# A hybrid transformer block on one core: weight buffers and normalised inputs that begin at different offsets

## The chip, the cores and the metric

The kernel runs on one core of a Trainium2 chip. The metric is the device time of one execution in microseconds. Three runs of the kernel before gave 820.04, 820.05 and 821.41 us, median 820.05 us. The profiled execution is a fourth one, of 820.38 us, and its trace spans 818.3 us from the first instruction to the last.

## The reference, cut to what matters

One block of a network for 512 tokens of width 1024, in float32. What counts here is which products of matrices there are; the rest hangs between them.

```python
u  = rms_norm(h, mix_norm_g)
z  = u @ w_in                              # 1024 -> 512 + 3*768 + 2*1024
y_a = s5_mixer(z[..., :512], ...) @ w_branch_a
y_b = dilated_attention(q, k, v) @ w_branch_b
h  = h + (g_a * y_a + g_b * y_b) @ w_out   # g_a, g_b: sigmoids of the last 2048 columns of z
u2 = rms_norm(h, ffn_norm_g)
gate = causal_depthwise_conv(u2 @ ffn_w_gate, ffn_conv_w, ffn_conv_b)
h  = h + (gelu(gate) * (u2 @ ffn_w_up)) @ ffn_w_down
u3 = rms_norm(h, ple_norm_g)
h  = h + sigmoid(u3 @ ple_w_gate) * (p @ ple_w_proj)
return rms_norm(h, final_norm_g)
```

## The kernel before

Activations lie with their features on the 128 partitions and the 512 tokens along the free axis; a width of 1024 is eight such slices (k = 0 to 7). The five engines work side by side and wait for one another by semaphores, which the tile framework places.

Each product is made in float32 accuracy out of three matmuls in the one-pass float32r format. Every operand is split into a high part, which is the value copied into a float32r tile, and a low part, which is what is left over. `mm3` (L148 to L151) then adds high times high (L149), high times low (L150) and low times high (L151) into one bank of PSUM. A matmul has a stationary operand of 128 columns, which TensorE loads first (the rows called PEld, LDWEIGHTS), and a moving operand that streams past it, here of 512 columns, in the last two output slices of 256.

Weights come in chunks of 1024 columns. `wprep` (L118 to L132) fetches one over SyncE's DMA queue into `wr`, ScalarE copies it into `wh` (L128), and VectorE subtracts into `wl` (L129). Each of the three has three buffers that are used in turn, and `wchunk` asks for the next chunk long before TensorE needs it. There are 130 chunks. The first 20 belong to the token-major products (`proj_tok`), in which the weights are the moving operand and the input `u1` is stationary: 24 matmuls a chunk, into tiles named `pa`. In the other 110 (`gemm`) 128 columns of weights are stationary and the activations move: eight weight tiles a chunk, three matmuls each. The last 16 weight tiles are used for two halves of the tokens, which adds 48. That makes 20 x 24 + 110 x 24 + 48 = 3168 matmuls of this kind, 3072 of them 512 columns wide and 96 of them 256 wide.

The normalised inputs `u1`, `u2` and `u3` share one set of four tiles (`u_tiles`, L153): `uh0` and `uh1` for the high parts, `ul0` and `ul1` for the low ones, each with four slices of 512 columns. `u_split` (L158) fills them. They are operands of `pa`, `v`, `gps` (the gates), `pg` and `pu` (the feed-forward block's two input products) and `eps` (the last gate). The other products read `mh`, `ml`, `ah`, `al`, `zh`, `zl`, `yh`, `yl`, `bx` and `px_`, which this kernel keeps in other slots; `zh` and `zl` reuse the slots of `uh0` and `ul0`.

All these tiles come out of two pools one behind the other, and their sizes per partition are whole multiples of 2048 bytes (8192 for a part of `u`, 4096 for a weight buffer). The order of allocation places them so that every one of those 3168 matmuls has both operands at the same distance, 64 bytes, past a multiple of 256 bytes. Slices within a tile start at multiples of 512 bytes and change nothing in that. An exception among the float32r matmuls are four others, in `rstd_full` (L241 and L242, twice): their stationary operand is `ones_r`, a small tile that lies 160 bytes past a multiple of 256, and 32 past a multiple of 64.

Between the products stand float32 matmuls (transposes, the recurrence's, attention), VectorE's work on the recurrence (`E`, `scr`), softmax, the convolution and the norms. None of it is touched.

Of the kernel before, what the change touches and what calls it, by code (L numbers as in the profile page):

```python
# [10 lines left out]
F32R = mybir.dt.float32r  # L11
# [6 lines left out]
P = 128  # L18
D = 1024
KD = D // P  # L20
SEQ = 512
# [22 lines left out]
STATS_AT = (7, 0)  # L44
NLAST = 2
LAST = ((0, 1), (2, 3))
LN2_HI = 0.693359375
LN2_LO = -2.12194440e-4

# [15 lines left out]
def tile_hybrid_block(ctx: ExitStack, tc: tile.TileContext, xT, xtok, pT, W, vecs, consts, ssm, out):  # L65
# [6 lines left out]
    ring = ctx.enter_context(tc.tile_pool(name="ring", bufs=3))  # L72
# [3 lines left out]
    def slot(i, shape, name, dt=F32):  # L76
        return sb.tile([P] + shape, dt, tag=f"s{i}", name=name)
# [10 lines left out]
    def t_tile(name):  # L88
        return ring.tile([P, 512], F32, tag="t", name=name, bufs=4)
# [22 lines left out]
    def wchunk():  # L112
        if ready:
            return ready.pop(0)
        with ahead():
            return wprep()

    def wprep(pieces=1, after=None):  # L118
        i = wpos[0]
        wpos[0] += 1  # L120
        raw = ring.tile([P, 1024], F32, tag="wr", name=f"wr{i}", bufs=3)
        hi = ring.tile([P, 1024], F32R, tag="wh", name=f"wh{i}", bufs=3)
        lo = ring.tile([P, 1024], F32R, tag="wl", name=f"wl{i}", bufs=3)
        n = 1024 // pieces
        for j in range(pieces):
            c = slice(j * n, (j + 1) * n)
            nc.sync.dma_start(raw[:, c], W[i][:, c])
            ACT.activation(hi[:, c], raw[:, c], AF.Copy)  # L128
            DVE.tensor_tensor(lo[:, c], raw[:, c], hi[:, c].bitcast(F32), op=ALU.subtract)  # L129
            if after and j == 0:  # L130
                after()
        return hi, lo  # L132
# [18 lines left out]
        PE.matmul(ps, st[1], mv[0], start=False, stop=last)  # L151

    def u_tiles(name):  # L153
        uh = [slot(f"uh{j}", [4, SEQ], f"{name}h{j}", F32R) for j in range(2)]
        ul = [slot(f"ul{j}", [4, SEQ], f"{name}l{j}", F32R) for j in range(2)]
        return ([uh[k // 4][:, k % 4, :] for k in range(KD)], [ul[k // 4][:, k % 4, :] for k in range(KD)])

    def u_split(u, k, src, gcol, c=slice(0, SEQ)):  # L158
# [13 lines left out]
    def first():  # L172
        for c in (slice(0, 128), slice(128, SEQ)):
            nc.sync.dma_start(x[:, 0, c], xT[:, 0, c])
            u_split(u, 0, x[:, 0, :], V_MIX, c)

    u = u_tiles("u1")
    ready.append(wprep(2, first))
    load_x(1)
    load_x(2)  # L180
    ready.append(wprep(2))
    load_x(3)
    nc.sync.dma_start(sp, ssm)
# [237 lines left out]
    def stt(o, a, s, b, o0, o1):  # L421
        DVE.scalar_tensor_tensor(o, a, s, b, op0=o0, op1=o1)

    def g_ssm():
# [12 lines left out]
        def rint(o, a, s):  # L437
            ts(o, a, s, ALU.mult, MAGIC, ALU.add)
            ts(o, o, -MAGIC, ALU.add)

        def exp_(o, a):
            xx, n, n1, r, q = e1, e2, e3, e4, e5
            ts(xx, a, -170.0, ALU.max, 170.0, ALU.min)
            rint(n, xx, LOG2E)
            stt(r, n, -LN2_HI, xx, ALU.mult, ALU.add)
            stt(r, n, -LN2_LO, r, ALU.mult, ALU.add)
# [448 lines left out]
    for m in range(4):  # L895
        ps = mm_tile("lps")
        gemm(ps, 4, (parts(yh, 4), parts(yl, 4)))
        t = t_tile("lg")
# [8 lines left out]
    h = slot("x", [KD, SEQ], "h")  # L907
# [21 lines left out]


    u2 = u_tiles("u2")
    acc2 = sb.tile([P, SEQ], F32, tag="acc", name="acc2")
    for m in range(KD):
# [11 lines left out]
    for part in range(2):  # L945
# [4 lines left out]
        for mi in range(HALF):  # L950
# [10 lines left out]
            t = t_tile("cv")  # L961
# [9 lines left out]
        if part == 1:  # L971
            u3 = u_tiles("u3")
            acc3 = sb.tile([P, SEQ], F32, tag="acc", name="acc3")
# [74 lines left out]
    waiting = []  # L1048
    for gi, rs in enumerate(LAST):
        c = slice(rs[0] * 128, rs[-1] * 128 + 128)  # L1050
        end = gi == len(LAST) - 1
        for m in tail:
# [19 lines left out]
    n = 0  # L1072
    for rs, y in zip(LAST, y4):
        for j in range(2):
# [153 lines left out]
```

## Time and profile before

| | |
|---|---|
| median of three runs | 820.05 us |
| the profiled execution | 820.38 us |
| its span | 818.3 us |
| TensorE busy (PE) | 801.2 us, 98% |
| weight loads (PEld) | 664.3 us, 81%, beside the matmuls |
| VectorE busy | 508.5 us, 62% |
| ScalarE busy | 346.4 us, 42% |
| mean granted TensorE clock | 0.987 |

A matmul is listed with the time from its start to its modelled end, 389 ns for 512 columns, and the next one starts before that end. So the pace of TensorE is read from the distance of two starts and not from the busy time.

### The profile page before, as it was taken

The numbers are of one execution on the slowest core, as the hardware profiler recorded it, in microseconds if no ns is written. First come the engines' busy times: TensorE is split into PE (matmuls) and PEld (weight loads), VectorE is DVE, ScalarE is ACT, GpSimd is POOL, SyncE is SP. The second block draws the span as 40 slices with busy tenths as digits, with TensorE's granted clock in tenths as the row PEclk, the third lists the DMA queues.
The fourth block names the chain that finished last, engine by engine and source line by source line (L and its number), as shares of the span: only waits on it lengthen the run. The fifth ranks groups of instructions, "written<-read, shape, count | busy, mean of one in ns | idle before, by whom it ended". The sixth has DMA issues, their size and how long they took to land.

```text
span 818.3 us, 10848 instructions
## 1 busy us (share of the span) xinstructions
PE 801.2 (98%) x4294; PEld 664.3 (81%) x4294; DVE 508.5 (62%) x944; ACT 346.4 (42%) x543; POOL 10.9 (1%) x10
## 2 busy tenths in 40 slices
PE   9999989799999999999999999999999999999996
PEld 7888868589777788888888888888888888888886
DVE  7963999992354447855776555332565556445586
ACT  6773632335344434344354433222344434335454
POOL 2001000000000000000000000000000000000000
PEclk9999998799999999999999999999999999999999
DMA  7731111122111123442322233223322332233202
GB/s 279 269 99 57 51 53 59 70 82 74 53 52 53 53 78 103 139 153 96 128 98 85 101 103 104 88 92 104 103 94 88 104 103 87 95 103 103 81 23 103
DMA packets 23810, 78.97 MB, mean 97 GB/s; under 512 B 2640, under 2 KB 3024, under 8 KB 23760
## 3 DMA queue, kind: packets, MB, share of 16 engines
q1 hardware_dynamic: 23616, 78.22, 28.2%
q8 instruction: 33, 0.54, 0.3%
q14 instruction: 17, 0.14, 0.1%
q10 hardware_dynamic: 144, 0.07, 0.0%
HBM read 76.18 MB, written 2.10 MB: 96 GB/s over the span
## 4 chain that ended last, share of the span: by engine, by line
PE 86%; DVE 10%; ACT 2%; issue 1%; DMA 0%; DVEq 0%; ACTq 0%
PE pg L151 5%; PE pu L151 5%; PE dps L150 5%; PE dps L151 5%; PE pu L150 5%; PE pu L149 5%; PE pg L150 5%; PE pg L149 5%; PE dps L149 5%; PE gps L149 4%; PE gps L151 4%; PE gps L150 4%; DVE E L413 3%; DVE scr L413 2%; PE pa L150 2%; PE pa L151 2%
## 5 line engine op out<-in xcount | busy, mean ns | idle before, releaser
L128 ACT ACTIVATE wh<-wr 128x1024 fp32r<-128x1024 f32 (+1 forms) x132 | 138.1, 1047 | 297.7 <-issue 61.6
L129 DVE TENSOR_TENSOR wl<-wr,wh 128x1024 fp32r<-128x1024 f32 (+1 forms) x132 | 160.0, 1213 | 68.2 <-ACT wh L128 67.9
L150 PE MATMUL pu<-u2l,wh 128*128 128x512 f32 x176 | 68.5, 389 | 0.0
L149 PE MATMUL pu<-u2h,wh 128*128 128x512 f32 x176 | 68.5, 389 | 0.0
L151 PE MATMUL pg<-u2h,wl 128*128 128x512 f32 x176 | 68.5, 389 | 0.0
L149 PE MATMUL pg<-u2h,wh 128*128 128x512 f32 x176 | 68.5, 389 | 0.0
L150 PE MATMUL pg<-u2l,wh 128*128 128x512 f32 x176 | 68.5, 389 | 0.0
L149 PE MATMUL dps<-ah,wh 128*128 128x512 f32 x176 | 68.5, 389 | 0.0
L150 PE MATMUL dps<-al,wh 128*128 128x512 f32 x176 | 68.5, 389 | 0.0
L151 PE MATMUL dps<-ah,wl 128*128 128x512 f32 x176 | 68.5, 389 | 0.0
L151 PE MATMUL pu<-u2h,wl 128*128 128x512 f32 x176 | 68.5, 389 | 0.0
L150 PE MATMUL pa<-wl,u1h 128*128 128x512 f32 x160 | 63.3, 396 | 0.4 <-DVE u1l L160 0.4
L149 PE MATMUL pa<-wh,u1h 128*128 128x512 f32 x160 | 63.5, 399 | 0.2 <-ACT u1h L159 0.2
L151 PE MATMUL pa<-wh,u1l 128*128 128x512 f32 x160 | 62.7, 394 | 0.0
L149 PE MATMUL gps<-u1h,wh 128*128 128x512 f32 x128 | 51.3, 401 | 0.0
L151 PE MATMUL gps<-u1h,wl 128*128 128x512 f32 x128 | 50.5, 394 | 0.0
L150 PE MATMUL gps<-u1l,wh 128*128 128x512 f32 x128 | 50.2, 392 | 0.0
L413 DVE TENSOR_TENSOR ext<-pg,n_y 128x512 f32<-128x512 f32 x22 | 15.2, 692 | 44.1 <-PE pg L151 44.1
L413 DVE TENSOR_TENSOR gt<-gps,n_bc 128x512 f32<-128x512 f32 x16 | 11.1, 693 | 47.0 <-PE gps L151 47.0
L150 PEld LDWEIGHTS pu<-u2l,wh 128*128 128x128 f32 x176 | 33.0, 188 | 6.9
L150 PEld LDWEIGHTS pg<-u2l,wh 128*128 128x128 f32 x176 | 33.0, 188 | 6.9
L149 PEld LDWEIGHTS dps<-ah,wh 128*128 128x128 f32 x176 | 33.0, 188 | 6.9
(304 smaller groups left out, 1566.1 us busy)
## 6 DMA issues: line engine op xcount, KB each, us to landing
wr<-in_W_dram SPq DMA_DIRECT2D x128, 512.0 KB, 3.2
xt<-in_xtok_dram SPq DMA_DIRECT2D x4, 512.0 KB, 7.9
h<-in_xT_dram SPq DMA_DIRECT2D x8, 256.0 KB, 4.9
out_dram<-fo SPq DMA_DIRECT2D x8, 256.0 KB, 2.3
x<-in_xT_dram SPq DMA_DIRECT2D x7, 256.0 KB, 5.6
wr<-in_W_dram SPq DMA_DIRECT2D x4, 256.0 KB, 5.5
cst<-in_consts_dram SPq DMA_DIRECT2D x1, 568.0 KB, 10.3
sp<-in_ssm_dram SPq DMA_DIRECT2D x1, 544.0 KB, 7.3
```

The lines of the kernel that those rows point to most:

```text
L128: ACT.activation(hi[:, c], raw[:, c], AF.Copy)
L129: DVE.tensor_tensor(lo[:, c], raw[:, c], hi[:, c].bitcast(F32), op=ALU.subtract)
L149: PE.matmul(ps, st[0], mv[0], start=first, stop=False)
L150: PE.matmul(ps, st[0], mv[1], start=False, stop=False)
L151: PE.matmul(ps, st[1], mv[0], start=False, stop=last)
L413: DVE.tensor_tensor(o, a, b, op=op)
```

## The change

The weight buffers `wh` and `wl` get 1088 columns in place of 1024, and the parts of `u` get 2112 in place of 2048. The data take 1024 (2048) of them from an offset that depends on the buffer: 0, 16 and 32 columns for the three `wh`, 48, 8 and 24 for the three `wl`, 0 and 32 for `uh0` and `uh1`, 16 and 48 for `ul0` and `ul1`. A column has 4 bytes. The room added is 256 bytes a tile, so that all tiles behind it move up by multiples of 256 bytes; the whole takes 2560 bytes a partition more. On each engine the instructions, their order and what they wait for are the same as before, row for row.

In bytes past a multiple of 256, the operands that moved stand so: `wh` at 64, 128 and 192 (in the order of the offsets 0, 16, 32), `wl` at 0, 96 and 160 (offsets 48, 8, 24), `uh0` at 64, `uh1` at 192, `ul0` at 128, `ul1` at 0. Of the 3168 matmuls 560 keep two operands at the same distance and 2608 don't any more. The two `wl` buffers at 96 and 160 lie 32 bytes past a multiple of 64; 696 of the matmuls read one of them. All other operands stay at multiples of 64.

```diff
+W_HI = (0, 16, 32)
+W_LO = (48, 8, 24)
+U_HI = (0, 32)
+U_LO = (16, 48)
...
-        hi = ring.tile([P, 1024], F32R, tag="wh", name=f"wh{i}", bufs=3)
-        lo = ring.tile([P, 1024], F32R, tag="wl", name=f"wl{i}", bufs=3)
+        hi = ring.tile([P, 1088], F32R, tag="wh", name=f"wh{i}", bufs=3)
+        lo = ring.tile([P, 1088], F32R, tag="wl", name=f"wl{i}", bufs=3)
+        hi = hi[:, W_HI[i % 3]:W_HI[i % 3] + 1024]
+        lo = lo[:, W_LO[i % 3]:W_LO[i % 3] + 1024]
...
-        uh = [slot(f"uh{j}", [4, SEQ], f"{name}h{j}", F32R) for j in range(2)]
-        ul = [slot(f"ul{j}", [4, SEQ], f"{name}l{j}", F32R) for j in range(2)]
+        def part(tag, nm, off):
+            t = slot(tag, [4 * SEQ + 64], nm, F32R)
+            return t[:, off:off + 4 * SEQ].rearrange("p (k n) -> p k n", k=4)
+
+        uh = [part(f"uh{j}", f"{name}h{j}", U_HI[j]) for j in range(2)]
+        ul = [part(f"ul{j}", f"{name}l{j}", U_LO[j]) for j in range(2)]
```

## Rows read from the trace of the kernel before

**Rows 1.** The page's first two parts: busy time, and the span in 40 slices.

```profile
span 818.3 us, 10848 instructions
PE 801.2 (98%) x4294; PEld 664.3 (81%) x4294; DVE 508.5 (62%) x944; ACT 346.4 (42%) x543; POOL 10.9 (1%) x10
...
PE   9999989799999999999999999999999999999996
```

**Rows 2.** Busy time by stretch: PE, PEld, DVE, ACT, POOL, clock, DMA.

```profile
100.00:200.00 100.00, 91.19 (x475) 76.72 (x474) 85.81 (x195) 36.11 (x55) 0.00 (x0) 0.91 0.22 74
...
300.00:400.00 100.00, 100.00 (x443) 82.69 (x442) 65.82 (x87) 41.33 (x55) 0.00 (x0) 1.00 0.37 121
...
500.00:600.00 100.00, 100.00 (x443) 82.81 (x442) 42.31 (x49) 28.06 (x34) 0.00 (x0) 1.00 0.29 96
```

**Rows 3.** Timeline, TensorE, output product: start, duration, engine, line, operation, out<-moving,stationary.

```profile
360.00 0.39 PE L149 MATMUL ops<-mh,wh 128*128 128x512 f32 x1
360.22 0.39 PE L150 MATMUL ops<-ml,wh 128*128 128x512 f32 x1
360.45 0.39 PE L151 MATMUL ops<-mh,wl 128*128 128x512 f32 x1
360.68 0.39 PE L149 MATMUL ops<-mh,wh 128*128 128x512 f32 x1
...
365.89 0.39 PE L151 MATMUL ops<-mh,wl 128*128 128x512 f32 x1
```

**Rows 4.** Timeline, TensorE, last gate with 256 columns: first and last of twenty.

```profile
803.08 0.28 PE L150 MATMUL eps<-u3l,wh 128*128 128x256 f32 x1
...
805.36 0.28 PE L151 MATMUL eps<-u3h,wl 128*128 128x256 f32 x1
```

**Rows 5.** Timeline, TensorE, around the matmuls with `ones_r` as stationary operand.

```profile
767.12 0.39 PE L151 MATMUL eps<-u3h,wl 128*128 128x512 f32 x1
767.35 0.39 PE L241 MATMUL n_ps<-n_hi,ones_r 128*128 128x512 f32 x1
767.58 0.39 PE L242 MATMUL n_ps<-n_lo,ones_r 128*128 128x512 f32 x1
767.81 0.40 PE L149 MATMUL eps<-u3h,wh 128*128 128x512 f32 x1
```

**Rows 6.** Timeline, weight loads at the same place.

```profile
766.90 0.19 PEld L151 LDWEIGHTS eps<-u3h,wl 128*128 128x128 f32 x1
767.13 0.19 PEld L241 LDWEIGHTS n_ps<-n_hi,ones_r 128*128 128x128 f32 x1
767.35 0.19 PEld L242 LDWEIGHTS n_ps<-n_lo,ones_r 128*128 128x128 f32 x1
767.58 0.19 PEld L149 LDWEIGHTS eps<-u3h,wh 128*128 128x128 f32 x1
```

**Rows 7.** Timeline, TensorE, runs of float32 matmuls of 128 columns.

```profile
77.95 1.28 PE L667 MATMUL es<-U,G 128*128 128x128 f32 x10
...
50.10 1.06 PE L261 MATMUL n_bps<-n_dg,ones 128*128 128x128 f32 x8
```

**Rows 8.** Groups by line and shape, VectorE and ScalarE: busy, mean ns.

```profile
L129 DVE TENSOR_TENSOR wl<-wr,wh 128x1024 fp32r<-128x1024 f32 x128 | 156.6, 1224 | 67.7 <-ACT wh L128 67.4
...
L413 DVE TENSOR_TENSOR ex<-ex 128x1024 f32<-128x1024 f32 x4 | 4.9, 1213 | 0.0
L413 DVE TENSOR_TENSOR ex<-sp,apw 128x1024 f32<-128x1024 f32 x4 | 4.8, 1220 | 0.8 <-PE es L667 0.8
...
L128 ACT ACTIVATE wh<-wr 128x1024 fp32r<-128x1024 f32 x128 | 135.6, 1060 | 296.0 <-issue 61.6 <-PE pg L150 59.3 <-PE dps L150 55.4
```

**Rows 9.** Line 129's instructions: count, shortest, median and longest in ns.

```profile
L129 DVE TENSOR_TENSOR wl<-wr,wh x132: 684/1225/1376, 4.7 to 790.7; 128x1024 fp32r<-128x1024 f32 x128, 128x512 fp32r<-128x512 f32 x4
```

**Rows 10.** The chain that ended last: first and last of ten pieces on line 129.

```profile
93.77 1.14 DVE wl L129
...
790.72 1.23 DVE wl L129
```

## The prediction

> **What bounds the kernel now.** Begin with the page's busy times: TensorE is busy for 801.2 of 818.3 us, in nearly every slice of the span [rows 1]. The table by stretch says where it isn't: between 100 and 200 us it misses 9 us, and from 300 us on it misses nothing, while VectorE is at 42 to 66 us in a hundred and ScalarE at 28 to 41 [rows 2]. So the time is the number of matmuls by the distance of their starts, and an edit that moves no instruction can pay or cost only through that distance, or through VectorE in the early stretch where TensorE waits.
>
> Next, the distance, from the timeline. From 360.00 to 365.89 us there are 26 distances, in all 5.89 us: 226.5 ns each [rows 3]. The three kinds of a triple (wh and mh, wh and ml, wl and mh) stand at 0.22 or 0.23 us alike, and a stretch with two thirds of the work on ScalarE and VectorE has the same 443 matmuls in 100 us [rows 2]. With 256 columns it is 2.28 us for 19 distances, 120.0 ns [rows 4]. The two widths give what a column costs, (226.5 - 120.0) / 256 = 0.416 ns, and what is left for each matmul whatever its width: 226.5 - 512 x 0.416 = 13.5 ns. This fixed part, 3168 x 13.5 ns = 42.8 us in the whole kernel, is all that other starting addresses could win on TensorE. The question of the case is whether it is a price of two operands at the same distance past 256 bytes, or one of changing the weights, whatever their address.
>
> **The change part by part.** Nothing is added, removed or moved on any engine: the same 3168 matmuls, 130 chunks, DMAs and waits. What can differ is how long one of four kinds of instruction takes.
>
> 1. *Matmuls whose operands no longer stand alike (2608), and the weight loads beside them.* The trace before has four matmuls that already are of that sort, those with `ones_r` as stationary operand (160 bytes past 256, where the moving operand is at 64). Around a pair of them the starts are at 767.12, 767.35, 767.58 and 767.81 us, 0.69 us for three distances, 230 ns each [rows 5]. Were the fixed part a collision of equal starting places, these distances should be near 213 ns, and the three should take 0.64 us; they take 0.69. The loads of `ones_r` are listed with 0.19 us like their neighbours [rows 6]. A second pair of rows has the same say for float32: `es` with both operands alike takes 1.28 us for ten, less the last one's 0.28 about 0.111 us each, and `n_bps`, whose stationary operand `ones` stands elsewhere (192 past 256, the moving one at 64), takes (1.06 - 0.28) / 7 = 0.111 us too [rows 7]. So I take 0 for this term. Its ends: at best the fixed part goes where operands differ, 2608 x 13.5 ns = -35.2 us; at worst each of the 2608 pays what the `ones_r` rows show beyond the usual, (690 - 3 x 226.5) / 3 = 3.5 ns, so +9.1 us. Rows 5 lie nearest, since they are of the same type and width, and their surplus is about what two starts rounded to 10 ns can feign.
>
> 2. *Matmuls that read a weight buffer 32 bytes past a multiple of 64 (696).* `ones_r` lies in just that way, and its load takes 0.19 us [rows 6]. I take 0; the end against it is 696 x 3.5 ns = +2.4 us, and below nothing there is no reason for a gain of its own.
>
> 3. *VectorE's and ScalarE's instructions that write the moved tiles (L128, L129, and the two of `u_split`).* Before, L129 has all three operands alike past 256 bytes and takes 1224 ns; instructions of the same size on operands that lie otherwise (`sp`, `apw`) take 1220, and one within a single tile 1213 [rows 8]. So 0. From 300 us on such a difference would be hidden behind TensorE, which never waits [rows 2]. It shows only where L129 stands on the chain that ended last, ten times [rows 10]. The bounds are the longest instruction of that line and the shortest mean above: 10 x (1376 - 1225) ns = +1.5 us [rows 9], 10 x (1213 - 1224) ns = -0.1 us.
>
> 4. *Everything behind the padded tiles*, which moves by multiples of 256 bytes: all of it keeps its distance past 256, so I take 0, and a cost of its own isn't in sight of any row; the +1.5 us of VectorE above is kept for both.
>
> The sum: 0. The profiled execution took 820.38 us, which is its span of 818.3 and 2.1 us around it, and this is 0.33 us over the median of the three runs. The forecast is 820.4 by the profile's own time and, on the scale of the median, 820.1 us.
>
> At term 1 a rule can be weighed. The trace has 226.5 ns from start to start. The Trainium skill, TensorE: Matmul & The Clock Gate, section Back-to-back issue gap, gives N / 2.4 + 2.5 ns for a warm gap, an estimate of 215.8 ns at 512 columns; the trace is 10.7 ns above it, and no row here reaches it. If what is above the rule were due to where the operands start, the 2608 matmuls would win some 27.9 us and the kernel would take about 792 us by that page. The same page, section Step-by-step: what each phase is for, says that weight loads have a read port of their own and take nothing from the running matmul, which speaks against that.
>
> **The rivals.**
>
> *The fixed part shrinks (faster).* For it: all 3168 matmuls have operands at the same place past 256 bytes, and the fixed part is so even (443 in 100 us, whatever the other engines do) that one cause must sit in all of them. The float32 rows show that less is possible: 111 ns at 128 columns leaves 5 ns, if a float32 row streams its columns twice (2 x 128 x 0.416 = 106.5 ns, an estimate) [rows 7]. With 5 in place of 13.5 ns for the 2608 matmuls it would be 22.2 us less, 798 us; if the fixed part went wholly, 785. Against it: rows 5, where operands stand apart and nothing is won, and the same evenness, since with 512-byte steps of the weights through a chunk a collision could well vary and doesn't.
>
> *A weight buffer off a multiple of 64 bytes costs (slower).* The mechanism: a load, or a stream, that starts in the middle of a 64-byte piece has one piece more to fetch, and the next matmul starts later by that. The place is L151 (and L150 of the `pa` products) for two of three chunks, 696 matmuls; the price is 3.5 ns each, so +2.4 us and 822.5 us. It decides from about 2.4 ns a matmul on, which is where 696 of them pass 1.64 us. For it: the 230 ns around `ones_r` [rows 5]. Against it: both matmuls there also wait for ScalarE's and VectorE's halves of their operands, which may be the 3 ns, and the load itself isn't longer [rows 6]. If instead every matmul whose operands differ paid it, the time would be 829.2 us.
>
> *The offsets don't do what they say.* 560 matmuls keep operands alike, and if what matters is a distance finer or coarser than 256 bytes, the change leaves the fixed part as it is. That ends where the forecast does, at 820.1.
>
> **How the numbers follow.** No effect, by terms 1 to 4 at nothing or by the rival before: 0.70. The fixed part shrinks, in whole or in part: 0.13 (785 to 815 us). The 696 matmuls cost: 0.10 (822.5). All 2608 cost, or VectorE and another mishap add up: 0.07 (823 to 829). A measurement of this kernel tells about 0.2% from no change, 1.64 us: the three runs lie 1.4 us apart. Faster by over 0.2% is the second case, 0.13, and a bit for chance, 0.14; slower is the last two, of which the first may fall within the bound, 0.16; the same 0.70. The range: no effect lies within 819 to 821.5 by the runs' spread; with the case of the 696 matmuls and two thirds of VectorE's end it reaches 823.5 (820.1 + 2.4 + 1.0), and I let it down to 817.6 for a small gain on a part of the matmuls. That leaves out the large gain and the large loss, under 2 in 10.
>
> **What would show it.** In the profile of the changed kernel the distance of the starts in the output product, the feed-forward products and the last gate should be 226.5 and 120.0 ns again, 443 matmuls in each full stretch of 100 us, the load of `wl` 0.19 us in all three buffers, L129 about 1224 ns. I am wrong if triples show unequal distances: L151 longer in two chunks of three says the slower rival, all starts at 215 to 219 ns say the faster one, and an unchanged pace with another total sends one to the stretch from 93 to 156 us, where VectorE leads.

## The result and the profile after

The changed kernel takes 832.87 us (median of four runs, 832.3 to 833.82) against 820.04 us before, a ratio of 1.0155 with a 95% interval of 1.0137 to 1.0172. It is 1.5% slower; the forecast was no change.

The page's first two parts of the kernel after, which answer to [rows 1]:

```profile
span 830.7 us, 10848 instructions
PE 813.3 (98%) x4294; PEld 662.7 (80%) x4294; DVE 508.4 (61%) x944; ACT 347.1 (42%) x543; POOL 10.9 (1%) x10
...
PE   9999989699999999999999999999999999999996
```

The span grew by 12.4 us and TensorE's busy time by 12.1; VectorE's and ScalarE's are what they were, and so is the number of instructions. The same three stretches as in [rows 2]:

```profile
100.00:200.00 100.00, 91.01 (x474) 75.40 (x473) 87.16 (x196) 37.14 (x55) 0.00 (x0) 0.95 0.23 74
...
300.00:400.00 100.00, 100.00 (x432) 80.99 (x431) 65.12 (x86) 39.80 (x53) 0.00 (x0) 1.00 0.36 121
...
500.00:600.00 100.00, 100.00 (x433) 80.96 (x432) 41.49 (x47) 27.57 (x33) 0.00 (x0) 1.00 0.29 96
```

In the two later stretches TensorE never waits and its granted clock is full (1.00), yet it begins 432 and 433 matmuls in 100 us where it began 443. So their starts lie farther apart. The timeline of the output product, for [rows 3], shows it:

```profile
363.65 0.39 PE L156 MATMUL ops<-mh,wh 128*128 128x512 f32 x1
363.88 0.39 PE L157 MATMUL ops<-ml,wh 128*128 128x512 f32 x1
364.11 0.39 PE L158 MATMUL ops<-mh,wl 128*128 128x512 f32 x1
364.33 0.39 PE L156 MATMUL ops<-mh,wh 128*128 128x512 f32 x1
...
369.65 0.39 PE L158 MATMUL ops<-mh,wl 128*128 128x512 f32 x1
```

26 distances take 6.00 us here, 230.8 ns each, after 226.5. Over all of this product the rows by tile (shortest, median and longest duration in ns, then the first and last start) are, before

```profile
L149 PE MATMUL ops<-mh,wh x64: 389/389/389, 347.8 to 390.6; 128*128 128x512 f32 x64
```

and after

```profile
L156 PE MATMUL ops<-mh,wh x64: 387/398/404, 350.4 to 394.3; 128*128 128x512 f32 x64
L157 PE MATMUL ops<-ml,wh x64: 388/394/401, 350.6 to 394.5; 128*128 128x512 f32 x64
```

What was one number has become a spread, and 63 triples take 43.85 us by the timeline where they took 42.84: 232.0 ns a matmul after 226.7. The same rows of the feed-forward block's first and the next product's first matmul tell where the 12.4 us are, before

```profile
L149 PE MATMUL pg<-u2h,wh x176: 389/389/389, 391.3 to 684.9; 128*128 128x512 f32 x176
...
L149 PE MATMUL pps<-px__5853,wh x16: 388/389/397, 750.8 to 761.2; 128*128 128x512 f32 x16
```

and after:

```profile
L156 PE MATMUL pg<-u2h,wh x176: 387/394/399, 395.0 to 694.8; 128*128 128x512 f32 x176
...
L156 PE MATMUL pps<-px__5853,wh x16: 388/397/399, 762.4 to 773.0; 128*128 128x512 f32 x16
```

From the first `pg` to the first `pps` it was 359.5 us and is 367.4: 7.9 us for 1584 matmuls, 5.0 ns each. Before `ops` begins the loss is 2.6 us (347.8 to 350.4), `ops` adds 1.0, and what follows `pps` 0.8. The 1104 matmuls before `ops` lose 2.4 ns each, half of what the feed-forward block loses. Why is not shown: TensorE's idle time in that part is 10.7 us before and 11.0 after, so the waits don't hide it, and from 100 to 200 us the granted clock was 0.91 before and 0.95 after, which helps the second trace by an amount that no run gives. Against [rows 8], L136 (the old L129) takes 1223 ns after 1224, and ScalarE's copy 1060 after 1060:

```profile
L136 DVE TENSOR_TENSOR wl<-wr,wh 128x1024 fp32r<-128x1024 f32 x128 | 156.5, 1223 | 70.6 <-ACT wh L135 70.4
```

### The profile page after: what moved, and what is told of

It reads as the page before. It is cut to its first block, busy times and chain, and to the rows that moved or that the text cites. A ratio compares the mean times of both kernels' runs of the same rounds, so it can differ in the third digit from the quotient of the medians.

```text
span 830.7 us, 10848 instructions
## 1 busy us (share of the span) xinstructions
PE 813.3 (98%) x4294; PEld 662.7 (80%) x4294; DVE 508.4 (61%) x944; ACT 347.1 (42%) x543; POOL 10.9 (1%) x10
## 4 chain that ended last, share of the span: by engine, by line
PE 85%; DVE 10%; ACT 2%; issue 1%; DMA 1%; DVEq 0%; SPq 0%; ACTq 0%
PE dps L157 5%; PE dps L156 5%; PE pu L158 5%; PE pu L156 5%; PE pg L156 5%; PE pg L158 5%; PE dps L158 5%; PE pg L157 5%; PE pu L157 5%; PE gps L156 4%; PE gps L158 4%; PE gps L157 4%; DVE E L424 3%; DVE scr L424 2%; PE pa L157 2%; PE pa L158 2%
## 5 line engine op out<-in xcount | busy, mean ns | idle before, releaser
L136 DVE TENSOR_TENSOR wl<-wr,wh 128x1024 fp32r<-128x1024 f32 (+1 forms) x132 | 159.2, 1207 | 71.5 <-ACT wh L135 71.3
L158 PEld LDWEIGHTS dps<-ah,wl 128*128 128x128 f32 x176 | 33.0, 188 | 8.1
L424 DVE TENSOR_TENSOR up<-pu,n_y 128x512 f32<-128x512 f32 x22 | 15.2, 691 | 39.6 <-PE pu L158 39.6
```

The costliest lines, as they stand in the source:

```text
L424: DVE.tensor_tensor(o, a, b, op=op)
```

## The experiments

Times are medians; each stands beside the kernel before on the same chip (819.9 to 820.8 us). "Pace" is the mean distance of the starts of two matmuls of 512 columns that follow each other, within a product or a chunk, from the timeline. Offsets are in columns of 4 bytes, and two operands are called in line when they start at the same place within 256 bytes. The two sweeps, the run with different offsets in `wh` and `wl` and the first run with four columns are one execution each (829.28, 825.84, 824.26 and 825.02 us); in these only the pace within the trace is read.

**The room alone.** As changed, but

```diff
-W_HI = (0, 16, 32)
-W_LO = (48, 8, 24)
-U_HI = (0, 32)
-U_LO = (16, 48)
+W_HI = W_LO = (0, 0, 0)
+U_HI = U_LO = (0, 0)
```

> The buffers get the 64 columns more, but all offsets are 0, so that operands move only by multiples of 256 bytes. Theory A (a matmul costs more when its moving operand and the stationary one that is loaded beside it start at different places within 256 bytes, about 12.4 us / 2608 = 4.8 ns each): 820 us, starts 226.6 ns apart as before. Theory B (the shift of the buffers by odd multiples of 256 bytes is what costs, the offsets do little): 829 to 833 us, starts 230 to 233 ns apart. Theory C (operands that begin 32 bytes past a multiple of 64 cost, 12.4 us / 696 = 18 ns each): 820 us.

Measured: 819.68 us, ratio 0.9988 (0.9977 to 1.0000), pace 226.7 ns in `ops`, `pg`, `pu` and `dps`. The shift by multiples of 256 bytes costs nothing; B falls.

**The weights' offsets alone** (`u_tiles` as before).

> Offsets and room for the weights' buffers alone, the normalised inputs as before. Theory A: five of six kinds of pair (2640 matmuls) start apart, 820 + 2640 x 4.8 ns = 832.7 us, in every product alike. Theory C: 832 us, but all of it at the matmuls that read wl from two chunks of three. Theory B: 829 to 833 us.

Measured: 834.18 us, ratio 1.0175 (1.0146 to 1.0205), pace 232.0 to 232.1 in all of `ops`, `pg`, `pu` and `dps`, and the matmuls that read `wl` are no slower than the others: in the products of 512 columns with stationary weights up to `pps` they take 230.9 ns to the next start, the other two of a triple 233.2 and 232.3. A, not C. It costs about as much as the whole change does (1.0155; the intervals overlap).

**The inputs' offsets alone** (`wprep` as before).

> Offsets and room for the normalised inputs alone, the weights as before. Theory A: the products that read them (480 pa, 48 v, 384 gps, 1056 pg and pu, 240 eps) pay for three of four parts, 1656 x 4.8 ns = 8 us, 828 us; ops, dps, bpa and the rest keep 226.6 ns. Theory C: 820 us, since no offset is off 64 bytes. Theory B: everything that lies behind the inputs moves by 1024 bytes and the parts by 256 each, 820 to 828 us.

Measured: 828.10 us, ratio 1.0101 (1.0072 to 1.0130). Busy time by stretch of this kernel, in the output product (360 to 390 us), in `pg` and `pu` (400 to 500) and in `dps` (520 to 560):

```profile
360.00:390.00 30.00, 30.00 (x134) 24.85 (x133) 17.61 (x22) 13.08 (x18) 0.00 (x0) 1.00 0.26 91
400.00:500.00 100.00, 100.00 (x433) 81.02 (x432) 63.91 (x79) 42.31 (x57) 0.00 (x0) 1.00 0.27 95
520.00:560.00 40.00, 40.00 (x178) 33.15 (x177) 11.85 (x12) 7.80 (x8) 0.00 (x0) 1.00 0.30 104
```

Only the products that read the moved inputs lose: 433 in 100 us, while 134 in 30 and 178 in 40 are the old pace. Every offset here is a multiple of 64 bytes; together with the run before, C falls.

**A sweep of offsets.** Weight buffers of 1152 columns, and an offset by the number of the chunk:

```diff
+        hi = hi_[:, W_OFF.get(i, 0):W_OFF.get(i, 0) + 1024]
+        lo = lo_[:, W_OFF.get(i, 0):W_OFF.get(i, 0) + 1024]
```

> The weights' buffers get 128 columns (512 bytes) more, so that their bases keep their place within 512 bytes, and each chunk of a product has an offset of its own, the same in wh and wl: 0 to 127 columns over the 44 chunks of pg and pu and others in gps, ops, dps and eps; offset 0 elsewhere. One chunk is 24 matmuls of pg, pu, gps, ops or eps. Theory A: chunks at offset 0 keep 226.6 ns from start to start, all others take 230 to 234 ns, by the distance within 256 bytes (so that 64 columns look like 0). Theory B: offset 0 is slow as well or nothing is. Theory C: only offsets that are not multiples of 16 columns are slow, by 6 ns a matmul on average (18 ns where wl is read). If a distance should make the starts closer than 226.6 ns, it is the one to build a faster kernel from; no theory expects it.

Measured, in `pg` and `pu` (the mean of the 23 distances within a chunk, over the two or four chunks with that offset):

| offset, columns | 0 | 1 | 2 | 4 | 8 | 16 | 24 | 32 | 48 | 64 | 96 | 112 | 126 | 127 |
|---|---|---|---|---|---|---|---|---|---|---|---|---|---|---|
| pace, ns | 227.0 | 232.3 | 230.7 | 233.3 | 233.2 | 233.2 | 234.0 | 232.8 | 229.3 | 227.6 | 232.3 | 229.3 | 233.3 | 226.7 |

In the timeline of `ops` a chunk's cost can be read off. These are the first matmul of a chunk with 8 columns and of the next one, then of a chunk with 64 and of the next:

```profile
358.95 0.39 PE L152 MATMUL ops<-mh,wh 128*128 128x512 f32 x1
...
364.54 0.40 PE L152 MATMUL ops<-mh,wh 128*128 128x512 f32 x1
...
381.23 0.39 PE L152 MATMUL ops<-mh,wh 128*128 128x512 f32 x1
...
386.68 0.40 PE L152 MATMUL ops<-mh,wh 128*128 128x512 f32 x1
```

5.59 us for 24 matmuls, 232.9 ns, and 5.45 us, 227.1 ns. So the offset matters by its place within 256 bytes, as A says, but not smoothly. No theory expected two things: 127 columns (4 bytes short of 512) are free right behind a slow chunk, and 4 columns are slow in `pg`, `pu` and `gps` and free in `ops` (226.7 ns). A run further down accounts for the second.

**More offsets** (44 others in the same place).

> The sweep with 44 further offsets (equal in wh and wl) in pg and pu. Theory R with a period of 256 bytes: offsets 60 to 68 are near 226.6 to 229 ns, all others 229 to 234. If any offset gives fewer than 226 ns, there is a distance better than none; I expect none, since 226.6 = 512 x 0.416 + 13.5 looks like the floor that equal places already reach.

Measured: 228.3 to 235.0 ns for 41 of the 44, and 226.7 to 226.8 for offsets 3, 30 and 63. None is below 226.6. Of R the period holds: 65, 66 and 68 take 232.2, 230.7 and 233.3 ns, as 1, 2 and 4 do within 0.2 ns. The rest of R fails: 61, 62, 65, 66 and 68 lie close to 256 bytes and take 230.7 to 233.3 ns. The chunks with 30 and 63 stand right behind slow ones and are free even so; that 30 is free fits no theory here. The chunk with 3 stood first, behind a product without offset, and may only have kept the pace that it found.

**All operands moved alike.**

```diff
+    small([16], "spacer")
     vec = small([V_N], "vec")
```

> The kernel before with one unused tile of 64 bytes a partition ahead of everything, so that all operands move alike, from 64 to 128 bytes past a multiple of 256, and no two of them come apart. Theory R (what costs is the distance between two operands): 820 us, starts 226.6 ns apart. Theory P (each operand has a good place of its own, 64 bytes past 256, and away from it a read takes longer): 3168 x about 6 ns, 835 to 840 us.

Measured: 820.18 us, ratio 1.0004 (0.9993 to 1.0016), pace 226.7 ns. R; moved by 64 bytes together, the operands cost nothing, so it is how they lie to each other that counts.

**One offset for all moved tiles.** As changed, but

```diff
+W_HI = W_LO = (32, 32, 32)
+U_HI = U_LO = (32, 32)
```

> The changed kernel with one offset, 32 columns, in all weight buffers and all parts of the inputs. Then the products that read the inputs (pa, v, gps, pg, pu, eps: 2208 matmuls) have both operands moved by 128 bytes, alike, and the other 960 (lps, bpb, bpa, ops, dps, pps) have them 128 bytes apart. Theory R: the first keep 226.6 ns, the others take 232.4 as offset 32 did in the sweep, 820 + 960 x 5.8 ns = 825.6 us. Theory P: all take 232, 838 us.

Measured: 826.04 us, ratio 1.0075 (1.0052 to 1.0098). Busy time by stretch, `pg` and `pu`, then `dps`:

```profile
400.00:500.00 100.00, 100.00 (x442) 82.83 (x442) 65.73 (x81) 43.10 (x59) 0.00 (x0) 1.00 0.28 96
520.00:560.00 40.00, 40.00 (x173) 32.20 (x172) 12.76 (x14) 7.41 (x7) 0.00 (x0) 1.00 0.26 92
```

442 in 100 us where weights and inputs moved together, 173 in 40 us where only the weights did (233.3 ns by the timeline). All moving operands of `dps` are alike and all its weights are, so it is the distance between the two kinds that costs, and not steps from one weight tile to the next. The Trainium skill, TensorE: Matmul & The Clock Gate, section Step-by-step: what each phase is for, has weight loads on a read port of their own that takes nothing from the running matmul. That gives no reason for a price on the distance between the two operands, and here 128 bytes cost 6.6 ns a matmul. Whether the load takes anything from the stream isn't shown, since no run parts the two.

**Different offsets in `wh` and `wl`.**

> As the sweep, but wh and wl of a chunk get different offsets, such as 0 and 32, in the 44 chunks of pg and pu; in the 8 chunks of ops both get 4 columns. A triple streams uh, ul, uh, past wh, wh, wl, and beside each stream the weights of the next matmul are loaded: wh, wl, and the next wh. Theory S (the stream and the load that runs beside it collide): with wl moved and wh not, it is the start after the second matmul of each triple (L153 to L154) that comes late, by 5 to 7 ns, and the other two keep 226.6; with wh moved and wl not, it is the other two. Theory O (a matmul is slow when its own two operands are apart): with wl moved alone, the start after the third (L154) is late. Theory N (steps between two loads in a row cost): with either moved, the two distances at which the offset changes are late, and the one between equal offsets is not. Offsets of 64 keep 226.6 ns. For the 4 columns in ops: 226.6 ns in all three buffers if it is the product, in one of three if it is the buffer.

Measured: the first chunk of `pg` has 0 in `wh` and 32 in `wl`. Its rows by line from 391.0 to 395.8 us (count, then shortest, median and longest duration in ns):

```profile
L154 PE MATMUL pg<-u2l,wh x8: 396/396/396, 390.7 to 395.5; 128*128 128x512 f32 x8
L155 PE MATMUL pg<-u2h,wl x8: 397/397/397, 390.9 to 395.8; 128*128 128x512 f32 x8
L153 PE MATMUL pg<-u2h,wh x7: 389/389/389, 391.2 to 395.3; 128*128 128x512 f32 x7
```

L153 has the duration of the kernel before, the other two are longer. The distances behind L153, L154 and L155 are 226.6, 232.4 and 234.3 ns in the mean of the chunk: free while `wh` is loaded beside a stream past `wh`, late while `wl` is loaded, and late while streaming past `wl`. With `wh` moved and `wl` not, all three are late (232.5, 232.9, 233.4). With 16 columns the pattern is another again (228.0, 228.6, 236.0; and 226.2, 236.0, 231.7). S, O and N each explain a part, and none all. Offsets 0 with 64, 4 and 127 are free here in either order (226.6 to 227.1 ns), and `ops` with 4 columns runs at 226.7 in all three buffers: not the buffer. In both places the 4 columns followed a chunk that was free.

**Four columns, and what came before.**

> 4 columns (16 bytes) gave 226.65 ns in ops and 233.4 ns in pg, pu and gps. Here wh and wl have 4 columns in the chunks of pg and pu, with three exceptions: 8 columns in the 12th chunk of the first half and in the first chunk of the second half, 0 columns in the 12th of the second half. Theory H (what came before counts: 4 columns keep the pace that they find): 226.7 ns in the first 11 chunks, 233 in the 12th and in the 10 after it; in the second half 233 in the first 11, 226.7 from the 12th to the end. Theory Q (the product counts: ops reads other tiles than pg and pu): 233 ns in all chunks of 4 columns. Theory D (only address and offset count, by the buffer's place): one of the three buffers differs from the others, all through both halves.

Measured, second half: 233.1 to 233.3 ns in the first 11 chunks, 226.7 in the 12th and in all that follow, though these have 4 columns again. The first matmuls of the last slow chunk, the chunk without offset, and the two after it:

```profile
630.44 0.40 PE L153 MATMUL pg<-u2h,wh 128*128 128x512 f32 x1
...
636.04 0.39 PE L153 MATMUL pu<-u2h,wh 128*128 128x512 f32 x1
...
641.48 0.39 PE L153 MATMUL pg<-u2h,wh 128*128 128x512 f32 x1
...
646.92 0.39 PE L153 MATMUL pu<-u2h,wh 128*128 128x512 f32 x1
```

5.60 us, 5.44 and 5.44: with the same offset, the same buffers in turn and the same product, a chunk costs 233.3 ns a matmul or 226.7, by what ran before it. H holds, Q and D fall. It also accounts for `ops` in the sweep, where the chunk ahead of the 4 columns had no offset and ran at 226.7 ns. In the first half H missed: only the first chunk ran at 227 ns, not eleven. Between it and the second stand the norm's two matmuls with `ones_r`, an earlier pair of the kind of [rows 5]:

```profile
391.08 0.39 PE L153 MATMUL pg<-u2h,wh 128*128 128x512 f32 x1
...
396.53 0.39 PE L245 MATMUL n_ps<-n_hi,ones_r 128*128 128x512 f32 x1
396.76 0.40 PE L246 MATMUL n_ps<-n_lo,ones_r 128*128 128x512 f32 x1
396.99 0.39 PE L153 MATMUL pu<-u2h,wh 128*128 128x512 f32 x1
...
402.59 0.39 PE L153 MATMUL pg<-u2h,wh 128*128 128x512 f32 x1
```

5.45 us before them, 5.60 after them.

**Four columns everywhere, and `ones_r` in line.**

```diff
-    ones_r = small([128], "ones_r", F32R)
+    ones_r = small([192], "ones_r", F32R)[:, 40:168]
```

> 4 columns in all 44 chunks of pg and pu, without exceptions, and the stationary tile of the norm's two matmuls, ones_r, moved by 40 columns so that it too starts 64 bytes past a multiple of 256. In the run before, the chunks of the first half fell to 233 ns right behind these two matmuls, which stand between the first and the second chunk. Theory H (4 columns keep the pace that they find, and it was ones_r that upset it): all 44 chunks at 226.7 ns, 820 us. If something else upset the first half, or 4 columns are slow in pu for another reason: 22 to 43 chunks at 233.3 ns, 24 x 6.7 ns = 0.16 us each, 823.4 to 827 us.

Measured: 819.65 us, ratio 1.0000 (0.9989 to 1.0011). All 176 matmuls of each kind in `pg` have one duration again:

```profile
L153 PE MATMUL pg<-u2h,wh x176: 389/389/389, 390.5 to 684.0; 128*128 128x512 f32 x176
```

All 44 chunks run at 226.7 ns. So it was `ones_r`: in the run before, two matmuls out of line upset the pace, and at a distance of 4 columns it stayed upset to the end of the first half.

**Offsets of 256 bytes.** As changed, with 0, 64, 0 and 64, 0, 64 in the weights, 0, 64 and 64, 0 in the inputs.

> The changed kernel with offsets of 0 or 64 columns (256 bytes) alone: 0, 64, 0 in wh, 64, 0, 64 in wl, 0, 64 and 64, 0 in the inputs. Theory R with a period of 256 bytes: 820 us, starts 226.6 to 227 ns apart. If unequal places as such cost: 830 us or more.

Measured: 819.73 us, ratio 0.9998 (0.9986 to 1.0009), pace 226.7 ns. Places that differ by 256 bytes are free.

## Why the prediction was wrong

What bounds the kernel was read rightly: only the distance of the starts could move the time, and it did. Terms 3 and 4 at nothing hold: L136 takes 1223 ns after 1224, and the room alone measures 819.68 us. Term 2 and its rival (32 bytes past a multiple of 64) are refuted: the inputs' offsets, all multiples of 64 bytes, cost 7 us alone, and with the weights' offsets alone the matmuls that read `wl` are no slower than the others.

The step that failed is term 1, taken as 0 where 12.8 us were measured, in two ways. First, its price. The rows around `ones_r` [rows 5] showed it, 230 against 226.5 ns, and I put these 3.5 ns down to rounding and to waits. In the run with four columns and `ones_r` in line, where this stretch has the same instructions and waits, the surplus is gone, 0.68 us for the three distances:

```profile
766.30 0.39 PE L155 MATMUL eps<-u3h,wl 128*128 128x512 f32 x1
766.53 0.39 PE L245 MATMUL n_ps<-n_hi,ones_r 128*128 128x512 f32 x1
766.75 0.39 PE L246 MATMUL n_ps<-n_lo,ones_r 128*128 128x512 f32 x1
766.98 0.39 PE L153 MATMUL eps<-u3h,wh 128*128 128x512 f32 x1
```

So it was the place of `ones_r`. In the kernel after, the same stretch reads

```profile
779.05 0.39 PE L158 MATMUL eps<-u3h,wl 128*128 128x512 f32 x1
779.28 0.40 PE L252 MATMUL n_ps<-n_hi,ones_r 128*128 128x512 f32 x1
779.52 0.39 PE L253 MATMUL n_ps<-n_lo,ones_r 128*128 128x512 f32 x1
779.75 0.40 PE L156 MATMUL eps<-u3h,wh 128*128 128x512 f32 x1
```

that is 233 ns, and now their neighbours have such distances too. The load's row of 0.19 us [rows 6], on which I leaned, can't show it: loads are listed at 0.19 us at either pace (PEld 662.7 us in all, after 664.3). What grows is the distance to the next start, and with it the listed duration of the matmul, whose end is modelled. Second, the count. I took 2608 matmuls whose own operands come apart; but the pace, once upset, passes on to others. The trace before shows that too, right behind the last of [rows 5]:

```profile
767.81 0.40 PE L149 MATMUL eps<-u3h,wh 128*128 128x512 f32 x1
768.04 0.40 PE L150 MATMUL eps<-u3l,wh 128*128 128x512 f32 x1
...
769.66 0.39 PE L151 MATMUL eps<-u3h,wl 128*128 128x512 f32 x1
...
770.34 0.39 PE L151 MATMUL eps<-u3h,wl 128*128 128x512 f32 x1
```

The eight distances behind `ones_r` take 1.85 us, 231 ns each, for matmuls whose own operands are in line; the next three take 0.68 us again. And after the change, in the products of 512 columns with stationary weights up to `pps`, the matmuls with operands in line take 231.6 ns to the next start and those out of line 231.8: the former were not spared. The upper end of the term, 2608 x 3.5 = 9.1 us, was therefore too low, where 5.0 ns on the 1584 matmuls of the feed-forward block gave 7.9 us alone. This case, "every matmul whose operands differ", stood among the rivals at 829.2 us and had a part of 0.07.

The float32 rows [rows 7] said nothing on it: they are of another type, and no run here tells whether places matter there. The faster rival was refuted rightly, and by the right rows: of 64 distances swept, none brought a chunk of 512 columns under 226.6 ns. The evenness of the pace before, which I read as a sign that places don't matter, went with equal places: it is there in each of the three runs in which all operands of the products are in line.

No version beats both kernels. With the operands in line, by moving all of them alike, by offsets of 256 bytes or by none, the time is 819.7 to 820.2 us, the time before.

## What to carry to other kernels

In a stream of float32r matmuls of 512 columns, each with its own weight load, let the moving and the stationary operands start at the same place within 256 bytes: here most other distances cost 4 to 8 ns on 227 for each matmul, and the whole change 1.5% of the kernel. A few distances were free (30, 63 and 127 columns), but only a measurement told which. In these traces a spread of the listed durations (387/398/404) at a full clock and without waits went with operands out of line, and a single value (389) with the pace of 226.7 ns; so such a spread is a reason to look at addresses. A few rows that differ from the rest by 3 ns are the experiment that the kernel has already made. Read on behind them until the pace is normal again, and explain them before putting them down to noise.

## What the runs showed that I had not expected

The pace has a memory. The same code at the same distance of 4 columns ran at 226.7 or at 233.3 ns over ten chunks, 240 matmuls, by the state in which it was found, and one chunk at distance 0 reset it.

The sign turns with the width. In the last gate's matmuls of 256 columns the kernel after is the faster one. Its best stretch has 25 distances in 2.95 us, 118.0 ns, against 120.0 before [rows 4]:

```profile
814.74 0.28 PE L157 MATMUL eps<-u3l,wh 128*128 128x256 f32 x1
...
817.69 0.28 PE L158 MATMUL eps<-u3h,wl 128*128 128x256 f32 x1
```

Over the 92 distances that no other work of TensorE lengthens it is 118.5 ns against 119.8, and the runs with the weights' or the inputs' offsets alone have 118.7 and 118.8. So the fixed part of 13.5 ns that I took for a floor is not one at 256 columns. Which of a matmul's two reads is delayed, why 30, 63 and 127 columns are free, and what holds the state between matmuls stay open: no run here separates the load from the stream.
